# Stage loads issued by SyncE in place of GpSimd, and no transferred Strassen sums in the last gate unit

## The chip, the cores and the metric

The kernel runs on one core of a Trainium2 chip. The time is the device time of one execution in microseconds; of the kernel before three runs took 2368.52 to 2370.82 us, with a median of 2368.99.

A core has five engines that run side by side: TensorE (PE in the profile, its weight loads PEld), VectorE (DVE), ScalarE (ACT), GpSimd (POOL) and SyncE (SP). Each takes its own instructions in order. A transfer is issued by an engine: SP and POOL do it here, each in the order of its own program, and an issue that has to wait for a buffer or for other data holds back everything behind it on that engine.

## The reference

One decoder block over 256 tokens of width 4096, in float32. A normed input is projected to 20480 columns; these feed a pooling branch, a gated convolution branch and two gates; the branches are projected back, gated, merged, projected once more, added to the input and normed:

```python
h = rmsnorm(x, norm_w[l])
proj = jnp.einsum('bsd,de->bse', h, w_in[l])
u_p, z_p, u_c, b_c, c_c, z_c, g_logit = jnp.split(proj, SPLIT_POINTS, axis=-1)
y_pool = causal_multiscale_pool(u_p, pool_w[l], pool_scale[l]) * jax.nn.silu(z_p)
y_conv = causal_gated_shortconv(u_c, b_c, c_c, conv_w[l], conv_b[l]) * jax.nn.silu(z_c)
ys = jnp.stack([y_pool, y_conv], axis=2)
br = jnp.einsum('bsnc,ncd->bsnd', ys, w_branch[l])
gates = jax.nn.sigmoid(g_logit.reshape(b, s, N_BRANCHES, d) + gate_b[l])
merged = jnp.sum(gates * br, axis=2)
x = x + jnp.einsum('bsd,de->bse', merged, w_out[l])
return rmsnorm(x, final_norm_w)
```

## The kernel before, in words

**Units and steps.** The columns of the three projections are worked off in units of 1024: twelve units of `w_in` for the two branches (names beginning with `c` and `p`; two of these also do the pooling), eight gate units `g0_0`, `g1_0`, ... `g0_3`, `g1_3`, eight branch units `b0_0`, `b1_0`, ... `b1_3`, and four output units `o0` to `o3`. A unit goes through its inner dimension in steps of 256 (16 steps for `w_in` and the output, 8 for a branch). Each step loads one block of weights, 128 partitions x 2048 values, into one of the three buffers of `raw` (a "weight load" below, SP, line 87).

Products are made in three parts from a high and a low part of each operand, so every block of weights is split: ACT copies it rounded into the `ring`, DVE subtracts that from the block and writes the low part beside it. There are two kinds of steps. A P step multiplies the blocks as they are, with 24 matmuls. An S step uses a Strassen-like scheme with 21 matmuls; for it DVE first makes sums of the blocks: `V` (two sums of 128x512 in one instruction of 128x1024) and `W`, which are split into the ring as well. `place_of_sum` and the table `HELPED` (line 625) take the sum V off DVE: for the S steps listed there under a unit's name, SP loads one summand into a free half of `E` or `R`, and POOL issues a second transfer that adds the other summand to it (`move_add`, line 94). Then only three quarters of the weights have to go to `raw` (1536 columns), since the first quarter is used only in that sum. An entry is taken only if a place is free in time.

**The order.** Matmuls, preparations and transfers are written down by one program that goes through the steps: `run_step` writes a step's matmuls, and behind each group of them `pump` (line 1222) writes down weight loads and splits as far ahead as buffers and ring allow, up to three steps. Every 6 matmuls a `tick` writes one item of `queue` (the ends of units: joining the partial sums, sigmoids, stores) and one item of the fills. The order on each engine is that in which the program writes it down.

**Fills and stages.** The left operands of the branch units (y) and of the output units (m, the merged branches) don't fit beside those of `w_in`. They are stored in DRAM (`y_d`, `m_d`), and as soon as a place of an earlier operand in `arena` is free, one is fetched. `Fill.fetch` (line 942) loads 128x512 values (256 KB) into a stage; at least 8 ticks (`LANDING`, line 963) later `pop_fill` (line 965) writes down its split into `arena`, a copy by ACT and a subtraction by DVE, for an S operand with four small sums by DVE before. The stages are the second half of `sa`, the tile `sb`, and until the second step of `b0_0` two quarters of `Y`. 19 such loads are of y: they begin in `g0_3` and most of them come in `g1_3` and `b0_0`, a few later; 12 are of m, from `b0_3` to the beginning of `o0`.

**The end of the last gate unit.** When an S unit's last S step is not its last step, its shared banks close early: the four instructions of `joins` (line 452) combine them in `R`, and then POOL adds the gate's bias (`gate_b`, 1024 KB to 128 partitions) to `R` by an adding transfer. `combine` (line 481) leaves 12 ticks and lets DVE add `E` to `R`. Of the gate units `g1_3` alone has its last S step before its last step.

In the profile nearly every DVE sum has line 72, every ACT copy line 69, SP's loads line 87, POOL's loads and stores line 91, and its adding transfers line 94; matmuls have line 1301. So the tiles' names tell the instructions apart.

Of the kernel before, what the change touches and what calls it, by code (L numbers as in the profile page):

```python
# [56 lines left out]
def hybrid_block(ctx: ExitStack, tc: tile.TileContext, x, x_t, norm_t, w_first, w_in, pool_w, pool_scale,  # L57
# [28 lines left out]
    def load(dst, src):  # L86
        return pin(nc.sync.dma_start(dst, src))  # L87

    def move(dst, src):

        return pin(nc.gpsimd.dma_start(dst, src))
# [72 lines left out]
    def flat(q):  # L164
        return q.rearrange("p o c -> p (o c)")
# [456 lines left out]

    few = NS_X - NB
    LAST_FIRST = ('cc0',)
    HELPED = {'cc0': (1, 2, 4, 5), 'cz0': (1, 2, 5), 'cb0': (1, 2, 4, 5, 7, 8), 'cu1': (1, 2, 4, 5, 7, 8), 'cc1': (1, 2, 4, 7, 8), 'cz1': (1, 2, 4, 5, 7), 'cb1': (1, 2, 4, 5), 'pz0': (1, 4, 5, 7), 'pu0': (1, 2, 4, 5, 7), 'pz1': (1, 4, 5, 6, 8), 'pu1': (1, 2, 4, 5, 7), 'g0_0': (1, 2, 4, 5, 7), 'g1_3': (1, 2, 5), 'g1_0': (1, 2, 4, 5, 8), 'g0_1': (1, 2, 4, 5, 6, 7), 'g1_1': (1, 4, 5, 7, 8), 'g0_2': (1, 2, 3, 4, 5, 7, 8), 'g1_2': (1, 2, 4, 5, 7, 8), 'g0_3': (1, 2, 4, 5, 7, 8), 'o0': (1, 2, 4, 5, 6), 'o1': (1, 2, 4, 5, 7), 'o2': (0, 1, 2, 4, 5), 'o3': (0, 2, 4, 5)}
    PLACES = {
# [308 lines left out]
    class Fill:  # L935
# [5 lines left out]

        def fetch(self, st):
            self.at, self.st = now[0], st
            move(flat(st), self.src)

        def fill(self):
            if self.o.kind == "P":
# [331 lines left out]
    for u in units:  # L1279
        for k, s in enumerate(t for t in u.steps if t.kind == "S"):  # L1280
            if k in HELPED.get(u.name, ()):
                helped.append(s)
# [315 lines left out]
```

## Time and profile before

| | |
|---|---|
| median of 3 runs | 2368.99 us (2368.52 to 2370.82) |
| the profiled execution | 2368.59 us |
| its span, first to last instruction | 2366.9 us |
| mean granted TensorE clock | 0.998 |
| PE busy | 2349.3 us (99%) |
| DVE busy | 2192.1 us (93%) |
| ACT busy | 1423.9 us (60%) |
| POOL busy | 138.3 us (6%) |
| transfers | 596.44 MB, 499.98 by SP's queue and 93.60 by POOL's |

The profile is of one execution. Its rows give the start of an instruction in us from the span's start, its duration, the engine, the line, the operation, what it writes and reads, and in brackets how long the engine was idle before it and what ended the wait. PE counts as busy while a matmul is under way; each overlaps the next, so that the spacing of their starts tells more than their durations. For a transfer the time to landing counts from its issue.

### The profile page before, as it was taken

To read this page: it belongs to the slowest core of one execution; us is meant where nothing else is said; L and a number is where in the kernel's file an instruction comes from. 1 tells how busy PE (TensorE), PEld (TensorE's weight loads), DVE (VectorE), ACT (ScalarE), POOL (GpSimd) and SP (SyncE) were. 2 spreads that over 40 slices of the span, in tenths; PEclk is the share of its full clock that TensorE was granted. 3 is DMA by queue.
4 is the path that set the end of the run, shared out by engine and by line. 5 is a ranking of instruction groups with operands and counts; after the bars stand their busy time and mean duration, and the time that the engine had idled before them with its cause. 6 is when DMAs were issued, how large, how long until landed. Compare 5 with 4: busy or idle time off the path is not lost.

```text
span 2366.9 us, 28142 instructions
## 1 busy us (share of the span) xinstructions
PE 2349.3 (99%) x10465; PEld 1943.7 (82%) x10465; DVE 2192.1 (93%) x2259; ACT 1423.9 (60%) x1481; POOL 138.3 (6%) x207
## 2 busy tenths in 40 slices
PE   9999999999999999999999999999999999999998
PEld 7888888888888888888888888888878888888886
DVE  8999999999999989989999999989899899899998
ACT  7565665656556656656666656565665566566555
POOL 0000000000001001000000000001100001000000
PEclk9999999999999999999999999999999999999999
DMA  8566678877777668656887898887866668778877
GB/s 337 179 235 212 242 273 255 262 238 232 258 260 244 226 226 253 232 211 229 273 284 246 276 284 258 257 307 243 273 230 233 243 241 282 250 229 286 264 244 274
DMA packets 107754, 596.44 MB, mean 252 GB/s; under 512 B 11424, under 2 KB 11680, under 8 KB 53984
## 3 DMA queue, kind: packets, MB, share of 16 engines
q1 hardware_dynamic: 84848, 499.98, 58.2%
q0 software_dynamic: 22336, 93.60, 16.7%
q8 instruction: 82, 1.34, 0.2%
q10 hardware_dynamic: 432, 1.07, 0.1%
q14 instruction: 56, 0.46, 0.1%
HBM read 562.09 MB, written 25.17 MB: 248 GB/s over the span
## 4 chain that ended last, share of the span: by engine, by line
PE 96%; DVE 2%; DMA 1%; ACT 1%; issue 0%; SPq 0%; DVEq 0%; ACTq 0%
PE sums L1301 70%; PE shared L1301 24%; PE shared L809 1%; DVE ring L72 1%; PE shared L528 1%; DMA raw<-in_w_in_dram 0%; ACT ring L69 0%; DVE R L72 0%; DMA raw<-in_w_out_dram 0%; DVE W L72 0%; PE shared L788 0%; SPq L87 0%; DVE V L72 0%; DVE arena L72 0%; PE shared L789 0%
## 5 line engine op out<-in xcount | busy, mean ns | idle before, releaser
L1301 PE MATMUL sums<-ring,arena 128*128 128x512 f32 x7551 | 1788.6, 390 | 4.7 <-DVE ring L72 2.5
L1301 PEld LDWEIGHTS sums<-ring,arena 128*128 128x128 f32 x7551 | 1414.2, 188 | 299.8 <-DVE ring L72 3.7
L72 DVE TENSOR_TENSOR ring<-raw,ring 128x1024 fp32r<-128x1024 f32 (+3 forms) x689 | 937.7, 1388 | 81.0 <-ACT ring L69 79.4
L69 ACT ACTIVATE ring<-raw 128x1024 fp32r<-128x1024 f32 (+3 forms) x689 | 794.3, 1186 | 234.5 <-PE sums L1301 126.9
L1301 PE MATMUL shared<-ring,arena 128*128 128x512 f32 x2556 | 646.9, 390 | 1.1 <-DVE ring L72 1.0
L1301 PEld LDWEIGHTS shared<-ring,arena 128*128 128x128 f32 x2556 | 480.5, 188 | 102.2 <-DVE ring L72 2.4
L69 ACT ACTIVATE ring<-W 128x1024 fp32r<-128x1024 f32 x213 | 226.3, 1062 | 396.3 <-DVE W L72 325.8
L72 DVE TENSOR_TENSOR ring<-W,ring 128x1024 fp32r<-128x1024 f32 x213 | 261.1, 1226 | 20.6 <-ACT ring L69 8.9
L69 ACT ACTIVATE ring<-V 128x1024 fp32r<-128x1024 f32 x154 | 163.1, 1059 | 171.8 <-DVE V L72 138.9
L72 DVE TENSOR_TENSOR V<-raw 128x1024 f32<-128x1024 f32 x154 | 187.8, 1219 | 10.4 <-DMA raw<-in_w_in_dram 7.6
L72 DVE TENSOR_TENSOR ring<-V,ring 128x1024 fp32r<-128x1024 f32 x154 | 187.8, 1219 | 3.5 <-ACT ring L69 3.5
L72 DVE TENSOR_TENSOR W<-W,raw 128x512 f32<-128x512 f32 x213 | 146.2, 687 | 0.0
L72 DVE TENSOR_TENSOR W<-V,raw 128x512 f32<-128x512 f32 x154 | 106.4, 691 | 4.6
L72 DVE TENSOR_TENSOR R<-R,E 128x1024 f32<-128x1024 f32 (+1 forms) x49 | 77.4, 1592 | 8.9 <-DMA R<-in_gate_b_dram 5.3
L94 POOL DMA_DIRECT2D E<-in_w_in_dram x34 | 29.5, 869 | 593.9 <-DMA E<-in_w_in_dram 311.5
L72 DVE TENSOR_TENSOR R<-R,shared 128x512 f32<-128x512 f32 x87 | 59.6, 685 | 2.2 <-ACT R L69 0.3
L69 ACT ACTIVATE arena<-sa 128x512 fp32r<-128x512 f32 (+2 forms) x49 | 25.5, 554 | 57.3 <-DVE sa L72 57.2
L72 DVE TENSOR_TENSOR ring<-E,ring 128x1024 fp32r<-128x1024 f32 x45 | 55.2, 1226 | 1.5 <-ACT ring L69 1.5
L69 ACT ACTIVATE E<-sums,rin 128x512 f32<-128x512 f32 x76 | 49.2, 681 | 11.7 <-PE sums L1301 11.7
L69 ACT ACTIVATE ring<-E 128x1024 fp32r<-128x1024 f32 x45 | 47.1, 1046 | 6.1 <-PE shared L1301 2.8
L72 DVE TENSOR_TENSOR W<-E,raw 128x512 f32<-128x512 f32 x41 | 28.3, 691 | 4.7 <-DMA E<-in_w_in_dram 2.3
L72 DVE TENSOR_TENSOR ring<-R,ring 128x1024 fp32r<-128x1024 f32 (+1 forms) x20 | 26.7, 1336 | 4.0 <-ACT ring L69 4.0
(146 smaller groups left out, 629.8 us busy)
## 6 DMA issues: line engine op xcount, KB each, us to landing
raw<-in_w_in_dram SPq DMA_DIRECT2D x267, 1024.0 KB, 4.9
raw<-in_w_branch_dram SPq DMA_DIRECT2D x64, 1024.0 KB, 5.4
raw<-in_w_out_dram SPq DMA_DIRECT2D x56, 1024.0 KB, 5.8
raw<-in_w_in_dram SPq DMA_DIRECT2D x51, 768.0 KB, 6.4
E<-in_w_in_dram SPq DMA_DIRECT2D x34, 512.0 KB, 7.1
E<-in_w_in_dram POOLq DMA_DIRECT2D x34, 512.0 KB, 9.4
R<-in_w_in_dram SPq DMA_DIRECT2D x17, 512.0 KB, 7.6
R<-in_w_in_dram POOLq DMA_DIRECT2D x17, 512.0 KB, 8.7
```

The costliest lines, as they stand in the source:

```text
L69: return pin(nc.scalar.activation(dst, src, func, **kw))
L72: return pin(nc.vector.tensor_tensor(out=dst, in0=a, in1=b, op=op))
L94: return pin(nc.gpsimd.dma_start(dst, src, accum_op=ALU.add))
L528: pin(nc.tensor.transpose(shared(j)[:, i * T + t * P:i * T + (t + 1) * P], src[:, t, c:c + P], ident))
L809: pin(nc.tensor.matmul(o, a[:, k, ts], b[:, k], start=(k, i) == (0, 0), stop=(k, i) == (3, 2)))
L1301: pin(nc.tensor.matmul(ps, lhs, rhs, start=n == 0, stop=n == u.total[b] - 1))
```

## The change

Two lines are changed. A fill's fetch is issued by SP (`load`) and no longer by POOL (`move`), for all 31 stage loads. And the table `HELPED` loses its entry for `g1_3`, so that all S steps of that unit have their sum V made by DVE and load whole blocks of weights. (The table stands on one line in the code.)

```diff
     HELPED = {'cc0': (1, 2, 4, 5),
...
               'g0_0': (1, 2, 4, 5, 7),
-              'g1_3': (1, 2, 5),
               'g1_0': (1, 2, 4, 5, 8),
...
         def fetch(self, st):
             self.at, self.st = now[0], st
-            move(flat(st), self.src)
+            load(flat(st), self.src)
```

`load` and `move` differ in the issuing engine alone:

```python
def load(dst, src):
    return pin(nc.sync.dma_start(dst, src))

def move(dst, src):

    return pin(nc.gpsimd.dma_start(dst, src))
```

More of the change, by code (lines that the diff above doesn't have):

```diff
@@ L624, in hybrid_block @@
     LAST_FIRST = ('cc0',)
-    HELPED = {'cc0': (1, 2, 4, 5), 'cz0': (1, 2, 5), 'cb0': (1, 2, 4, 5, 7, 8), 'cu1': (1, 2, 4, 5, 7, 8), 'cc1': (1, 2, 4, 7, 8), 'cz1': (1, 2, 4, 5, 7), 'cb1': (1, 2, 4, 5), 'pz0': (1, 4, 5, 7), 'pu0': (1, 2, 4, 5, 7), 'pz1': (1, 4, 5, 6, 8), 'pu1': (1, 2, 4, 5, 7), 'g0_0': (1, 2, 4, 5, 7), 'g1_3': (1, 2, 5), 'g1_0': (1, 2, 4, 5, 8), 'g0_1': (1, 2, 4, 5, 6, 7), 'g1_1': (1, 4, 5, 7, 8), 'g0_2': (1, 2, 3, 4, 5, 7, 8), 'g1_2': (1, 2, 4, 5, 7, 8), 'g0_3': (1, 2, 4, 5, 7, 8), 'o0': (1, 2, 4, 5, 6), 'o1': (1, 2, 4, 5, 7), 'o2': (0, 1, 2, 4, 5), 'o3': (0, 2, 4, 5)}
+    HELPED = {'cc0': (1, 2, 4, 5), 'cz0': (1, 2, 5), 'cb0': (1, 2, 4, 5, 7, 8), 'cu1': (1, 2, 4, 5, 7, 8), 'cc1': (1, 2, 4, 7, 8), 'cz1': (1, 2, 4, 5, 7), 'cb1': (1, 2, 4, 5), 'pz0': (1, 4, 5, 7), 'pu0': (1, 2, 4, 5, 7), 'pz1': (1, 4, 5, 6, 8), 'pu1': (1, 2, 4, 5, 7), 'g0_0': (1, 2, 4, 5, 7), 'g1_0': (1, 2, 4, 5, 8), 'g0_1': (1, 2, 4, 5, 6, 7), 'g1_1': (1, 4, 5, 7, 8), 'g0_2': (1, 2, 3, 4, 5, 7, 8), 'g1_2': (1, 2, 4, 5, 7, 8), 'g0_3': (1, 2, 4, 5, 7, 8), 'o0': (1, 2, 4, 5, 6), 'o1': (1, 2, 4, 5, 7), 'o2': (0, 1, 2, 4, 5), 'o3': (0, 2, 4, 5)}
     PLACES = {
```

## The prediction

> **What bounds the kernel now.** I read the page first, then the busy time by stretches of 60 us, and then the instructions in order of time where PE was idle, engine by engine.
>
> ```profile
> PE 2349.3 (99%) x10465; PEld 1943.7 (82%) x10465; DVE 2192.1 (93%) x2259; ACT 1423.9 (60%) x1481; POOL 138.3 (6%) x207
> ```
>
> PE is the engine that is full. The stretches tell where it isn't:
>
> ```profile
> core 0 of [0], span 2366.9 us
> core 0: us, PE busy (x) PEld busy (x) DVE busy (x) ACT busy (x) POOL busy (x), PEclk, DMA share, GB/s
> 1560.00:1620.00 60.00, 60.00 (x266) 49.71 (x265) 53.12 (x51) 36.09 (x38) 4.68 (x6) 1.00 0.79 257
> 1620.00:1680.00 60.00, 58.41 (x254) 46.96 (x253) 52.04 (x62) 36.36 (x40) 5.72 (x10) 1.00 0.74 260
> 1680.00:1740.00 60.00, 56.40 (x239) 45.63 (x238) 51.35 (x65) 35.10 (x44) 5.53 (x9) 0.97 0.75 262
> 1740.00:1800.00 60.00, 60.00 (x274) 49.89 (x273) 57.10 (x54) 34.11 (x37) 2.60 (x5) 1.00 0.62 218
> ```
>
> Of the span of 2366.9 us PE is idle for 17.6. A full stretch holds 266 wide matmuls, 0.226 us each. Apart from the first and the last microseconds of the program, PE falls behind only between 1620 and 1740, that is in the last gate unit `g1_3` and the first branch unit `b0_0`, where the stages of y are fetched. What PE does there:
>
> ```profile
> 1649.08 2.48 PE L1301 MATMUL shared<-ring,arena 128*128 128x512 f32 x9
> ...
> 1659.41 2.81 PE L1301 MATMUL sums<-ring,arena 128*128 128x512 f32 x11 [0.49 <-DVE ring L72]
> ```
>
> ```profile
> 1717.56 2.20 PE L1301 MATMUL sums<-ring,arena 128*128 128x512 f32 x9
> 1721.22 0.50 PE L1301 MATMUL sums<-ring,arena 128*128 128x512 f32 x1 [1.46 <-ACT ring L69]
> 1723.74 0.83 PE L1301 MATMUL sums<-ring,arena 128*128 128x512 f32 x2 [2.02 <-DVE ring L72]
> 1724.38 4.44 PE L1301 MATMUL shared<-ring,arena 128*128 128x512 f32 x12
> 1728.65 1.55 PE L1301 MATMUL sums<-ring,arena 128*128 128x512 f32 x6
> ```
>
> First stall: 34 matmuls start between 1649.08 and 1659.41 and need 34 x 0.226 = 7.7 us; they took 10.3, so 2.6 are lost, all waiting for DVE. Second stall: 24 matmuls from 1717.56 to 1728.65 need 5.4 and took 11.1, so 5.7 are lost. Part of these is clock:
>
> ```profile
> 1720.82:1724.24 3.42, 1.00 (x3) 0.63 (x4) 3.42 (x5) 3.42 (x5) 0.53 (x1) 1.00 0.17 72
> 1724.24:1727.65 3.41, 3.41 (x10) 2.63 (x9) 3.41 (x5) 3.41 (x6) 0.00 (x0) 0.50 0.88 322
> ```
>
> After 3.4 us with PE busy for 1.0 the clock is granted at 0.50 for 3.41 us, which costs half of that, 1.7. So the second stall is 4.0 of waiting and 1.7 of clock. These 8.3 us are all that better fetching can win.
>
> **Why DVE is late there.** DVE's waits for transfers, in order of time:
>
> ```profile
> 1636.29 1.02 DVE L72 TENSOR_TENSOR sa<-sa 128x128 f32<-128x128 f32 x4 [3.71 <-DMA sa<-y_d]
> ...
> 1703.89 1.23 DVE L72 TENSOR_TENSOR R<-R,E 128x1024 f32<-128x1024 f32 x1 [5.25 <-DMA R<-in_gate_b_dram]
> ```
>
> 3.71 us go to a stage load, the fourth of y's, called the late load below; 5.25 to the gate's bias, which a DMA adds to R. Before the first stall stands the one, before the second the other. POOL, which issues both, tells why the stage load is late:
>
> ```profile
> 1624.50 0.90 POOL L94 DMA_DIRECT2D E<-in_w_in_dram  x1 [12.44 <-DMA E<-in_w_in_dram]
> 1625.07 0.89 POOL L91 DMA_DIRECT2D sa<-y_d  x1
> ```
>
> POOL stood 12.44 us at the adding transfer for the Strassen sum of `g1_3`, whose first half SyncE was still loading, and the stage load was queued behind it.
>
> **The change, part by part.** On POOL, from the end of `g0_3` on (one piece of the difference; E is the place of the Strassen sum):
>
> ```order
>  L94 DMA R<-in_w_in_dram 128x1024
> -L91 DMA sa<-y_d 128x512
>  L94 DMA R<-in_gate_b_dram 128x2x1024
> -L91 DMA sa<-y_d 128x512
> -L91 DMA sb<-y_d 128x512
> -L94 DMA E<-in_w_in_dram 128x1024
> -L91 DMA sa<-y_d 128x512
>  L91 DMA gates_d<-R 128x2048
> ```
>
> The blocking transfer and all stage loads leave; R's bias and the gate's store remain. Only one of the three entries for `g1_3` was ever taken, so one transfer pair goes. On SP at the same place, before and then changed:
>
> ```order
> L87 DMA raw<-in_w_in_dram 128x1536
> L87 DMA raw<-in_w_in_dram 128x2048 x8
> L87 DMA E<-in_w_in_dram 128x2x512
> L87 DMA raw<-in_w_in_dram 128x2048 x3
> L87 DMA raw<-in_w_in_dram 128x1536
> ```
>
> ```order
> L87 DMA raw<-in_w_in_dram 128x2048
> L87 DMA sb<-y_d 128x512
> L87 DMA raw<-in_w_in_dram 128x2048 x2
> L87 DMA sa<-y_d 128x512
> L87 DMA Y<-y_d 128x512
> L87 DMA raw<-in_w_in_dram 128x2048
> ```
>
> The late load (the `sa` here) now follows two weight loads, and the `x1536` weight behind E becomes a whole one. On DVE one piece:
>
> ```order
> +L72 TENSOR_TENSOR V<-raw 128x1024
>  L72 TENSOR_TENSOR arena<-sb,arena 128x512
> -L72 TENSOR_TENSOR W<-E,raw 128x512
> -L72 TENSOR_TENSOR ring<-raw,ring 128x3x512
> -L72 TENSOR_TENSOR W<-W,raw 128x512
> -L72 TENSOR_TENSOR ring<-E,ring 128x2x512
> +L72 TENSOR_TENSOR W<-V,raw 128x512
> ```
>
> One sum is DVE's again; the rest only reads V for E. Its price, and the durations of the transfers concerned (whole page, then the window 1687 to 1706):
>
> ```profile
> L72 DVE TENSOR_TENSOR V<-raw 128x1024 f32<-128x1024 f32 x154 | 187.8, 1219 | 10.4 <-DMA raw<-in_w_in_dram 7.6
> ```
>
> ```profile
> R<-in_gate_b_dram POOLq DMA_DIRECT2D x7, 1024.0 KB, 12.5
> ```
>
> ```profile
> raw<-in_w_branch_dram SPq DMA_DIRECT2D x4, 1024.0 KB, 10.3
> R<-in_gate_b_dram POOLq DMA_DIRECT2D x1, 1024.0 KB, 16.1
> ```
>
> Step 1, the late load: SP can issue it when DVE has split the stage's last contents, at 1622.6, and DVE wants it at 1636.29 - 3.71 = 1632.6. (The first row is DVE's; the others are transfers of the window 1606 to 1636.)
>
> ```profile
> 1621.95 0.68 DVE L72 TENSOR_TENSOR arena<-sa,arena 128x512 fp32r<-128x512 f32 x1
> ```
>
> ```profile
> sa<-y_d POOLq DMA_DIRECT2D x2, 256.0 KB, 9.5
> sb<-y_d POOLq DMA_DIRECT2D x2, 256.0 KB, 12.2
> ```
>
> With 9.5 us it lands at 1632.1, in time; with 12.2 DVE waits 2.2. DVE gains between 1.5 and 3.7; I take 3.71, since fewer bytes move there than before (E's two transfers of 512 KB go, 256 KB of weights come).
>
> Step 2, the added sum: DVE loses 1.22. Net 2.49 at 1650. PE waits directly for DVE there, so 2.5 of the first stall's 2.6 go.
>
> Step 3, three stage loads on POOL shared the DMA engines with weights that ACT then waited for, and DVE for ACT:
>
> ```profile
> 1661.48 0.54 POOL L91 DMA_DIRECT2D sb<-y_d  x1
> 1662.02 1.06 POOL L91 DMA_DIRECT2D Y<-y_d  x2
> ```
>
> ```profile
> 1674.19 1.23 DVE L72 TENSOR_TENSOR ring<-raw,ring 128x1024 fp32r<-128x1024 f32 x1 [1.39 <-ACT ring L69]
> ```
>
> ```profile
> ACT ring L69 <- DMA raw<-in_w_branch_dram: 6.7, 3, 3.9
> ```
>
> (The last is of ACT's waits from 1660 to 1705.) In the new order on SP these three come after the third weight of the branches, so the first weights are ahead of them:
>
> ```order
> L87 DMA raw<-in_w_branch_dram 128x2048 x3
> L87 DMA sb<-y_d 128x512
> L87 DMA Y<-y_d 128x512 x2
> L87 DMA raw<-in_w_branch_dram 128x2048 x2
> L87 DMA sa<-y_d 128x512
> ```
>
> Before, SP had only the 64 weights in a row there. DVE's 1.39 goes (bounds 0 and 1.39). So DVE finishes R 2.49 + 1.39 = 3.88 us earlier, and POOL, which issues the bias then, does it at 1683.9:
>
> ```profile
> 1687.75 1.23 POOL L94 DMA_DIRECT2D R<-in_gate_b_dram  x1 [1.31 <-DVE R L72]
> ```
>
> Step 4, the bias transfer: between the usual 12.5 us and this place's 16.1. No stage load stands around it in POOL's queue any more, but SP's queue beside it stays full. I take the middle, 14.3; DVE gains another 1.8, 5.7 in all.
>
> Step 5, the second stall: its 4.0 us of waiting shrink by what DVE gains over PE, 5.7 - 2.5 = 3.2, to 0.8. The first stall, 2.6 us in several pauses, left the clock at 1.00 (stretch 1620 above), so I take the 1.7 us of half clock as gone (bounds 0 and 1.7).
>
> Step 6, at nothing: SP's issues and waits for the 31 loads (19 of y, 12 of m). In 1540 to 1760 SP waits almost always, for DVE to free a weight buffer:
>
> ```profile
> SPq L87 <- DVE W L72: 106.5, 18, 12.8
> SPq L87 <- DVE ring L72: 95.7, 24, 8.3
> ```
>
> A stage load waits for a DVE instruction that stands earlier in the program than the one the next weight load waits for, so it is let through first. If that cover failed, the weights behind it would be late (third rival). The loads of m come where ACT itself waits for PE to free the ring (window 1940 to 2060), so PE has its lead and their 256 KB each cost nothing:
>
> ```profile
> ACT ring L69 <- PE sums L1301: 17.6, 11, 3.7
> ```
>
> Sum: 2.5 + 3.2 + 1.7 = 7.4 us. The profiled execution took 2368.59 (span 2366.9 and 1.7 around it), 0.4 under the median of 2368.99. So 2361.2 against it, 2361.6 against the median.
>
> **The rivals.** First, the bias lands no sooner. For it: the DMA engines are full there (10.3 us for a weight against a median of 4.9 for the page's 267 of `w_in`), and few bytes go.
>
> ```profile
> raw<-in_w_in_dram SPq DMA_DIRECT2D x267, 1024.0 KB, 4.9
> ```
>
> Then DVE gains 3.88, the second stall keeps 4.0 - 1.4 = 2.6 of waiting, and the clock may still drop: 2.5 + 1.4 = 3.9 us, 2365.1. The Trainium skill (DMA: Bandwidth & Descriptors, Issuing engines are not separate DMA queues) says that transfers of all issuing engines run on the same 16 engines, and that issuing from several saves only the issuing time. By that rule this rival would be the outcome; the full engines agree with it, of the 12.44 us block in POOL's order it does not speak.
>
> Second, the change doesn't free DVE: on SP the late load stands behind two weight loads, and if it takes 12.2 us, DVE still waits 2.2 and with the added sum gains 0.3. For it speaks the crowd of that stretch, against it that the crowd shrinks. If step 3 fails too, the stalls stay nearly whole: 2368.7.
>
> Third, slower: SP holds the weights at a stage load whose buffer isn't free. POOL did:
>
> ```profile
> 1698.94 0.54 POOL L91 DMA_DIRECT2D sb<-y_d  x1 [8.98 <-DVE arena L72]
> ```
>
> In the new order this load stands before the tenth weight of the branches. If SP stands 9.0 us there and nothing covers it, PE loses 9.0 less the 2.5 gained: 2368.99 + 6.5 = 2375.5. It decides from a hold of 7.2 us on (2.5 + 4.7); against it is that SP waits for DVE there anyway.
>
> **How the numbers follow.** My forecast (5 to 8.3 us won) has 0.57, the first rival 0.17, the second 0.12, the third 0.14. 0.2% is 4.7 us, about what a measurement of this kernel can tell from no change. A little of the first rival, where the clock holds, counts as faster (3.9 + 1.7): faster 0.60, same 0.26, slower 0.14. The low end is all 8.3 us gone (2360.7) and one more for what I read off by tenths; the high end takes in the first two rivals and as much again: 2359.6 to 2369.5. The forecast's own range is 2359.9 to 2364.2.
>
> **What would show it.** Right: DVE's 3.71 wait for the stage is gone, POOL has no 12 us wait at E, PE's waits before 1660 vanish, the clock stays at 1.00 near 1720, DVE's wait for the bias is under 4 us. Wrong: ACT waits for weights grow beyond 6.7 us between 1660 and 1705, or new waits of PE from 1740 on.

## The result, and the profile after

The changed kernel takes 2361.11 us (2360.6 to 2362.27), the kernel before on the same chip 2368.99 (2368.52 to 2370.88). The ratio is 0.9965, with a 95% interval of 0.9954 to 0.9976: faster by 7.9 us, forecast were 7.4. The profiled execution took 2360.96 us, its span is 2359.2.

The page's line on the engines, after. DVE has one instruction more, the sum `V`, and POOL 32 fewer: 31 stage loads and one adding transfer.

```profile
PE 2346.9 (99%) x10465; PEld 1943.4 (82%) x10465; DVE 2192.6 (93%) x2260; ACT 1424.7 (60%) x1481; POOL 121.0 (5%) x175
```

The stretches of 60 us, after. PE was busy for 58.41 and 56.40 us in them before; now both are full, and the second is back at a clock of 1.00:

```profile
1620.00:1680.00 60.00, 60.00 (x266) 49.47 (x265) 57.07 (x68) 40.53 (x46) 0.59 (x1) 1.00 0.69 258
1680.00:1740.00 60.00, 59.98 (x264) 49.03 (x263) 53.71 (x65) 33.67 (x41) 2.31 (x3) 1.00 0.74 259
```

PE's waits over the whole program, after. Both rows lie in the first 100 us of the program; behind these PE has no wait left that the view shows:

```profile
PE shared L1065 <- DVE rout L1070: 1.1, 1, 1.1
PE sums L1301 <- DVE ring L72: 0.3, 1, 0.3
```

At the place of the second stall PE's timeline, after, shows no bracket, and twelve matmuls take 2.9 us where they took 4.44 at half clock. Only the group of twelve ahead of them is still a little late: from its start to the next one's are 3.01 us (1714.81 to 1717.82), and 12 x 0.226 are 2.7, so 0.3 are lost in gaps too short for a bracket.

```profile
1714.81 3.17 PE L1301 MATMUL sums<-ring,arena 128*128 128x512 f32 x12
1717.82 2.90 PE L1301 MATMUL shared<-ring,arena 128*128 128x512 f32 x12
1720.56 8.78 PE L1301 MATMUL sums<-ring,arena 128*128 128x512 f32 x38
```

The cause, in the timelines of SP, DVE and POOL, after. SP issues the late load at 1622.87; DVE takes it at 1632.81 without a wait (no bracket), and still waits 2.54 us for the gate's bias, where it waited 5.25:

```profile
1622.87 0.33 SPq L87 DMA_DIRECT2D sa<-y_d  x1
...
1632.81 1.01 DVE L72 TENSOR_TENSOR sa<-sa 128x128 f32<-128x128 f32 x4
...
1684.14 1.17 POOL L94 DMA_DIRECT2D R<-in_gate_b_dram  x1 [61.06 <-ACT ring L69]
...
1697.40 1.23 DVE L72 TENSOR_TENSOR R<-R,E 128x1024 f32<-128x1024 f32 x1 [2.54 <-DMA R<-in_gate_b_dram]
```

**A measure inside the trace.** The profile of a second execution of the changed kernel (number 11 below) has a span of 2361.8 us against 2359.2, a difference larger than some experiments are to tell, and part of it lies at the start and the end. So the tables below use a stretch of PE's work that all these kernels share: from the group of nine matmuls near 1614, ahead of all the changes, to the last group of the program. Before (first fence) it takes 2355.36 - 1613.69 = 741.67 us, after (second fence) 2347.53 - 1614.00 = 733.53. That is 8.1 us less, and the two stalls had been read as 8.3.

```profile
1613.69 2.20 PE L1301 MATMUL shared<-ring,arena 128*128 128x512 f32 x9
...
2355.36 0.88 PE L1534 MATMUL shared<-ring,arena 128*128 128x256 f32 x6
```

```profile
1614.00 2.20 PE L1301 MATMUL shared<-ring,arena 128*128 128x512 f32 x9
...
2347.53 0.88 PE L1534 MATMUL shared<-ring,arena 128*128 128x256 f32 x6
```

PE had lost another 0.4 us between the two stalls, in gaps too short for a bracket. The same 171 matmuls there, before (first fence) and after (second fence):

```profile
1674.30 39.34 PE L1301 MATMUL sums<-ring,arena 128*128 128x512 f32 x171
```

```profile
1671.97 38.92 PE L1301 MATMUL sums<-ring,arena 128*128 128x512 f32 x171
```

### The profile page after: what moved, and what is told of

It is laid out like the page before. It is cut to its first block, busy times and chain, and to the rows that moved or that the text cites. A ratio compares the mean times of both kernels' runs of the same rounds, so it can differ in the third digit from the quotient of the medians.

```text
span 2359.2 us, 28140 instructions
## 1 busy us (share of the span) xinstructions
PE 2346.9 (99%) x10465; PEld 1943.4 (82%) x10465; DVE 2192.6 (93%) x2260; ACT 1424.7 (60%) x1481; POOL 121.0 (5%) x175
## 4 chain that ended last, share of the span: by engine, by line
PE 99%; DMA 0%; DVE 0%; SPq 0%; ACT 0%; issue 0%; DVEq 0%
PE sums L1301 72%; PE shared L1301 25%; PE shared L809 1%; PE shared L528 1%; DMA raw<-in_w_in_dram 0%; PE shared L788 0%; SPq L87 0%; PE shared L789 0%; PE shared L791 0%; SPq L162 0%; DVE ring L72 0%; ACT ring L69 0%; ACT V L69 0%; PE shared L790 0%; PE sums L1534 0%
```

## The experiments

Eleven kernels in three groups, each group beside the kernel before on one chip (its medians there: 2369.48, 2367.91 and 2370.06 us). "Gain" is by the measure above; the last two columns are the transfer of `g1_3`'s bias and DVE's wait for it.

| kernel | median us | ratio to before, interval | gain | bias | DVE waits |
|---|---|---|---|---|---|
| before | 2368.99 | | | 16.1 | 5.3 |
| changed | 2361.11 | 0.9965 [0.9954, 0.9976] | 8.1 | 13.2 | 2.5 |
| 1 table alone | 2365.71 | 0.9987 [0.9978, 0.9996] | 2.7 | 16.0 | 5.0 |
| 2 queue alone | 2361.3 | 0.9969 [0.9958, 0.9981] | 8.4 | 14.2 | 2.4 |
| 3 add later | 2365.09 | 0.9982 [0.9973, 0.9991] | 4.1 | 15.9 | 5.3 |
| 4 no bias | 2363.39 | 0.9975 [0.9966, 0.9984] | 4.1 | none | none |
| 5 m on POOL | 2361.6 | 0.9969 [0.9957, 0.9982] | 6.5 | 14.3 | 3.7 |
| 6 one ahead of the bias | 2362.4 | 0.9973 [0.9962, 0.9985] | 7.2 | 14.6 | 3.5 |
| 7 four near 1660 | 2363.47 | 0.9978 [0.9969, 0.9988] | 6.3 | 13.7 | 4.1 |
| 8 add later, no bias | 2360.54 | 0.9964 [0.9951, 0.9977] | 8.9 | none | none |
| 9 one behind the bias | 2363.07 | 0.9969 [0.9958, 0.998] | 6.4 | 15.0 | 4.3 |
| 10 four around the bias | 2364.51 | 0.9979 [0.9969, 0.9988] | 6.0 | 15.8 | 4.4 |
| 11 changed, again | 2361.8 | 0.9966 [0.9952, 0.998] | 7.1 | 14.1 | 3.4 |

The last row sets the scale: the changed kernel's own two profiles differ by 1.1 us in the gain, the later arrival of the bias among it. The gain is of one execution each. By the medians the kernels gain up to 2.0 us more or less than this column says (kernel 4: 6.1, kernel 7: 4.4), so a difference of one or two microseconds between two rows isn't shown by the column alone.

### The two parts alone

**1, the table alone**: the entry of `g1_3` goes, all stage loads stay on POOL.

```diff
-    HELPED = {..., 'g0_0': (1, 2, 4, 5, 7), 'g1_3': (1, 2, 5), 'g1_0': (1, 2, 4, 5, 8), ...}
+    HELPED = {..., 'g0_0': (1, 2, 4, 5, 7), 'g1_0': (1, 2, 4, 5, 8), ...}
```

> The table's entry for g1_3 is gone, the stage loads stay on POOL. My theory: the 12.44 us wait of POOL goes and with it DVE's 3.71, less 1.22 for the added sum, so the first stall (2.6 us of PE) nearly vanishes. Three stage loads still share the engines with the branch weights near 1660, DVE keeps its 1.39, and the bias still follows a stage load and takes about 16 us, so the second stall of 5.7 stays: 2366.5 us. Rival (what counts is E's bytes, which crowd the DMA engines): loads and bias get faster everywhere, nearly the whole gain, about 2361.5 us. Rival (only the queue counts): 2369.

Measured: a gain of 2.7 us, about the first stall. POOL's hold at E is gone and with it DVE's wait for the late load. The second stall stays, and behind it a stretch of half clock. PE's waits in this kernel; the first two are the second stall, the other two lie ahead of all the changes:

```profile
PE sums L1301 <- DVE ring L72: 2.0, 1, 2.0
PE sums L1301 <- ACT ring L69: 1.3, 1, 1.3
PE shared L1065 <- DVE rout L1070: 1.1, 1, 1.1
PE shared L1301 <- DVE ring L72: 0.4, 1, 0.4
```

**2, the queue alone**: SP issues the stage loads, the table keeps its entry.

```diff
-            move(flat(st), self.src)
+            load(flat(st), self.src)
```

> All 31 stage loads are issued by SP, the table keeps g1_3, so the Strassen sum still goes through E. My theory: the late load no longer stands behind the adding transfer, DVE gains its 3.71 without paying 1.22, the bias has POOL's queue to itself: both stalls vanish, 2361 us, at most 0.5 from the changed kernel. Rival (bytes): as many bytes as before move, the crowd stays, most of the gain is missing, 2367. Rival (the rule that the issuing engine saves only issuing time): 2369.

Measured: the whole gain, 8.4 us. POOL stands at the adding transfer as before, even a little longer, but no stage load is queued behind it. POOL's timeline in this kernel:

```profile
1621.20 0.91 POOL L94 DMA_DIRECT2D E<-in_w_in_dram  x1 [13.10 <-DMA E<-in_w_in_dram]
1622.45 0.57 POOL L91 DMA_DIRECT2D gates_d<-R  x1 [0.34 <-issue]
1682.70 1.19 POOL L94 DMA_DIRECT2D R<-in_gate_b_dram  x1 [59.68 <-DVE R L72]
```

So the two parts don't add: both free the late load, 2.7 and 8.4 against 8.1 together. Once SP issues the loads, nothing measurable is left for the table's entry to give.

### The first stall's cause by itself

**3, add later**: the kernel before, in which POOL's adding transfer for E is written down a few weight loads later. In POOL's order this one row moves, to behind the late load, the gate's store and two more stage loads (three loads in all, not four as the expectation has it). No transfer is added, removed or put on another engine.

```diff
-                    adding.append((state["nl"] + WAIT, t, v, w[:, NH:3 * NH]))
+                    adding.append((state["nl"] + (4 if t.host.name == "g1_3" else WAIT), t, v, w[:, NH:3 * NH]))
```

> The kernel before with one row moved on POOL: the adding transfer of g1_3 is issued three places later in SP's order, so four stage loads and a store stand ahead of it in place of behind it. Same transfers, same engines, same bytes. My theory (the order of POOL's queue makes the late load late): DVE's 3.71 goes, the first stall goes, the second stays or is a little shorter: 2366.4 us. Rivals (bytes, or the queue's kind): no change, 2369.

Measured: 4.1 us. The hold at E, the 3.71 us and the first stall are gone with the order alone. It is 1.4 more than table alone gains: there DVE makes the added sum, at 1.22 us, here it doesn't. (By the medians the two are only 0.6 apart.) What is left is the second stall, some 0.8 us shorter (PE waits 0.62 us for ACT in it, before 1.46), and its half clock, by windows of 3.4 us in this kernel:

```profile
1716.94:1720.36 3.42, 1.16 (x4) 0.76 (x5) 3.42 (x5) 3.42 (x5) 0.54 (x1) 1.00 0.26 72
1720.36:1723.77 3.41, 3.41 (x10) 2.63 (x9) 3.41 (x5) 3.41 (x7) 0.00 (x0) 0.50 0.85 329
```

### The second stall's cause by itself

**4, no bias**: the kernel before without `g1_3`'s bias transfer.

```diff
-        more = [] if u.added is None or not early else [lambda: move_add(u.dst, u.added)]
+        more = [] if u.added is None or not early or u.name == "g1_3" else [lambda: move_add(u.dst, u.added)]
```

> The kernel before without the adding transfer of the gate's bias in g1_3 (this unit's bias is left out). My theory (the bias' landing sets the second stall): DVE's 5.25 us wait goes, down to the 2 us or so for which the weights are late there too; the second stall's 4.0 us of waiting go to 1 or less and the half clock with them; the first stall stays at 2.6: 2363.8 us. Rival (the second stall comes from the first, or from late weights): DVE waits for the weights as long, 2368.5 us.

Measured: 4.1 us. The second stall and the half clock are gone. The first stall stays, and in this execution it is longer: 46 matmuls from 1646.85 to 1661.43 need 46 x 0.226 = 10.4 us and took 14.6, so 4.2 are lost in place of 2.6 (DVE waited 4.25 us for the late load here, and 1.02 for a weight ahead of it). That is why the gain stays below the 5.7 of the second stall; the profiled execution, 2364.98 us, is also 1.6 slower than the kernel's median. PE's waits in this kernel; the 2.2 and 0.5 of the 0.8 are the first stall, the rest is from the first 100 us of the program:

```profile
PE shared L1301 <- DVE ring L72: 2.2, 2, 1.2
PE shared L1065 <- DVE rout L1070: 1.1, 1, 1.1
PE sums L1301 <- DVE ring L72: 0.8, 2, 0.5
```

**8, add later and no bias**: both edits together, all stage loads still on POOL.

> The kernel before with the adding transfer of the Strassen sum issued three places later and without the bias transfer of g1_3 (this unit's bias is left out); all stage loads on POOL. My theory (the two stalls have these two causes and no third): both stalls go, 2361 us with all loads on POOL. Rival (POOL's stage loads themselves cost): 2363 or more.

Measured: 8.9 us, which are the 8.3 of both stalls, the 0.4 between them and 0.2 that aren't placed. That kernels 3 and 4 apart give nearly as much, 4.1 + 4.1 = 8.2, is chance: kernel 3 gains some of the second stall too, and kernel 4 loses by its longer first one. PE's waits in this kernel, both from the first 100 us of the program:

```profile
PE shared L1065 <- DVE rout L1070: 1.1, 1, 1.1
PE sums L1301 <- DVE ring L72: 0.2, 1, 0.2
```

The stalls have these two causes and no third; and a better arrival of the bias could give the changed kernel at most about a microsecond more, which these runs wouldn't tell from nothing.

### Which of the moved loads matter

The next five are the changed kernel with some loads back on POOL. Four count the fetches and pick some by number (5 picks by operand):

```diff
-            load(flat(st), self.src)
+            fetched.append(self); (move if len(fetched) in (8, 9, 10, 11) else load)(flat(st), self.src)
```

**5, m on POOL**: the 12 loads of m (`(load if self.o not in m_ops else move)`).

> The changed kernel with the twelve loads of m back on POOL. My theory (step 6: they are covered by PE's lead on either queue): no difference, 2361.1 us, within 0.5. Rival (part of the gain is made by m's loads): 2363 or more.

Measured: 2361.6. PE has one wait of 0.3 us after 1740, so for m the issuing engine costs nothing that this run shows. Most of the 1.6 us less of gain lies at the bias, which landed later here (PE waits 1.1 us for DVE at 1718), as in the second profile of the changed kernel, though nothing near it was edited.

**7, four near 1660** (fetches 8 to 11, as in the diff).

> The changed kernel with the four stage loads near 1660 us back on POOL, none of them near the bias. My theory (step 3): they share the engines with the first branch weights again, ACT waits for a weight near 1670, DVE loses the 1.39 us, the bias is issued 1.2 later, PE waits 1.2 at the second stall: 2362.3 us, or 2364 if the half clock follows. Rival (these loads cost nothing wherever they are): 2361.1, and the 1.39 came from elsewhere.

Measured: 2363.47, gain 6.3: between the two expected times, with the clock at 1.00 throughout. DVE's waits for ACT tell step 3 directly. First the two waits of this kernel, then the one that the changed kernel has there:

```profile
1671.38 1.23 DVE L72 TENSOR_TENSOR ring<-raw,ring 128x1024 fp32r<-128x1024 f32 x1 [1.35 <-ACT ring L69]
1675.71 1.23 DVE L72 TENSOR_TENSOR ring<-raw,ring 128x1024 fp32r<-128x1024 f32 x1 [1.04 <-ACT ring L69]
```

```profile
1674.56 1.23 DVE L72 TENSOR_TENSOR ring<-raw,ring 128x1024 fp32r<-128x1024 f32 x1 [1.03 <-ACT ring L69]
```

Kernels 1 and 3, whose loads are on POOL, have both (1.31 and 1.35 us for the first); kernel 2, whose loads are on SP, has the second alone. The 1.39 us of the kernel before belong to these loads. ACT's waits for branch weights say the same, more loosely: 6.5 us from 1660 to 1705 here, 3.8 and 5.0 in the two profiles of the changed kernel.

**6, one ahead of the bias** (fetch 13, which POOL issues just before it).

> The changed kernel with one stage load back on POOL, the one that stands directly ahead of the bias there. My theory (a stage load ahead of the bias in its own queue makes it late, step 4): the bias takes 15 to 16 us in place of 13.2, DVE waits 2 us longer for it, and since the changed kernel has no reserve at the second stall PE waits 2 us, with the half clock 3.7: 2363 to 2364.8 us. Rival (the bias is slow from SP's weights beside it and from nothing else): 13 us and 2361.1.

Measured: 14.6 us for the bias, 2362.4. It went less far than expected: one load ahead of the bias isn't what makes 16 us.

**9, one behind the bias** (fetch 14), **10, four around the bias** (fetches 12 to 15, two on each side), and **11, the changed kernel again** beside them.

> The changed kernel with one stage load back on GpSimd: the 14th fetch, the Y load that GpSimd issues right behind the gate bias of g1_3. It cannot delay the bias's issue (about 1684). If a stage load that GpSimd issues behind the bias stretches its transfer, the bias takes 15 us or more, the VectorE wait for it rises from 2.5 to about 4.5 us, TensorE waits 1 to 2 us and the time is 2362 to 2363.5. If it does not, the bias takes 13.2 to 14.3 us as with all loads on SyncE, and the time is 2361.2.

> The changed kernel with the four stage loads around the gate bias of g1_3 (two ahead of it, two behind it) back on GpSimd. If the 16 us of the bias in the kernel before come from these neighbours on its own queue, the bias takes 15.5 to 16.1 us here, VectorE waits about 5 us for it, TensorE waits 2 to 3 us near 1718, perhaps with the half clock behind it, and the time is 2363.5 to 2366. If the queue does not matter, the bias takes 13.2 to 14.6 us and the time is 2361.2 to 2362.4.

> The changed kernel once more, beside the two others on the same chip, as their measure: 2361.1 within 0.6, the bias 13.2 to 14.3 us.

Transfers issued from 1682 to 1688, in the order 9, 10, 11 (the last column is the time to landing in us):

```profile
R<-in_gate_b_dram POOLq DMA_DIRECT2D x1, 1024.0 KB, 15.0
...
Y<-y_d POOLq DMA_DIRECT2D x1, 256.0 KB, 16.0
```

```profile
R<-in_gate_b_dram POOLq DMA_DIRECT2D x1, 1024.0 KB, 15.8
...
Y<-y_d POOLq DMA_DIRECT2D x1, 256.0 KB, 15.9
```

```profile
R<-in_gate_b_dram POOLq DMA_DIRECT2D x1, 1024.0 KB, 14.1
Y<-y_d SPq DMA_DIRECT2D x1, 256.0 KB, 12.1
```

Kernels 9 and 10 came as the first of their two expectations has it; the time of kernel 11 lies 0.1 us beyond the 0.6 that it was given. With four stage loads back around it, the bias is at 15.8 us, nearly what it took with all of them on POOL (15.9 to 16.1); with one behind, at 15.0; with none near it on POOL, 13.2 to 14.3 over five profiles (the changed kernel's two and kernels 2, 5 and 7). So the neighbours on the bias's own queue make it slow. (POOL also issues three of the four up to 1.1 us earlier than SP does, `Y` at 1685.62 in kernel 10 and at 1686.67 in the changed kernel; this is not separated from the queue.) PE's longest waits in the middle, in the order 9, 10, 11, follow the arrival:

```profile
1719.21 0.73 PE L1301 MATMUL sums<-ring,arena 128*128 128x512 f32 x2 [1.80 <-DVE ring L72]
```

```profile
1719.55 0.74 PE L1301 MATMUL sums<-ring,arena 128*128 128x512 f32 x2 [2.01 <-DVE ring L72]
```

```profile
1718.11 0.73 PE L1301 MATMUL sums<-ring,arena 128*128 128x512 f32 x2 [0.89 <-DVE ring L72]
```

The ratios of 10 and 11 to the kernel before overlap in their intervals. Compared with each other, on one chip, the two do differ: seven of the nine runs of kernel 10 take longer than each of the five of kernel 11, and the medians are 2.7 us apart. By what way a neighbour slows the bias, through the descriptors that POOL writes or through the order in which the queue is served, was not told apart.

## Why the prediction was right

The time came 0.5 us under the forecast, inside the forecast's own range, and none of the rivals came about. By its steps:

**Steps 1 to 3** can be tested together, since each shifts the moment at which DVE is done with R and POOL issues the bias. Counted from the fixed group of matmuls near 1614, the issue comes earlier than before by:

| kernel | by the steps | measured |
|---|---|---|
| changed | 3.71 - 1.22 + 1.39 = 3.88 | 3.92 |
| table alone (steps 1 and 2) | 3.71 - 1.22 = 2.49 | 2.58 |
| add later (step 1) | 3.71 | 3.84 |
| queue alone (steps 1 and 3) | 3.71 + 1.39 = 5.10 | 5.15 |
| four near 1660 (steps 1 and 2) | 3.71 - 1.22 = 2.49 | 2.50 |

For the changed kernel the measured number is (1687.75 - 1613.69) - (1684.14 - 1614.00) = 3.92; the others come from the same two rows of their traces. Each step has the size that was read off the profile before, to about 0.1 us. (Kernels 5, 9 and 11 have 3.9 like the changed one; 6 and 10 have 4.3, and why is open.) Of step 1, the late load's own time of 6.8 us was better than the 9.5 taken, with no effect, since 9.5 was in time already.

**Step 4** is the term that was mis-sized: 14.3 us for the bias was a middle between two rows, and it took 13.2 in the profile. The reason given, that no stage load stands around it in POOL's queue any more, is what kernel 10 shows. Over five profiles it took 13.2 to 14.3, so the value taken lies at the slow end of what the kernel does. Counted from the fixed group, DVE came to the sum of R and E (1703.89 - 1613.69) - (1697.40 - 1614.00) = 6.8 us earlier than before, where 5.7 were forecast.

**Step 5** followed from it: 0.8 us of waiting were to remain at the second stall, 0.3 did, in the group of twelve shown above. In the second profile, with the bias at 14.1 us, the wait is the 0.89 quoted above. The 1.7 us of half clock went, as taken. Against the forecast's 7.4, the 8.1 of the trace are these 0.5 and the 0.4 between the stalls, less some 0.2 of small delays elsewhere. So the prediction had it wrong that the 8.3 us of the two stalls are all that better fetching can win. That the median came within 0.5 us of the forecast is in part luck: the two profiles of the changed kernel differ by 1.1 us, and by as much the bias missed the value taken.

**Step 6** held: PE has no wait after 1740, and SP's order didn't make PE wait for weights. SP did wait for DVE's splits into `arena`, which free the stages, six times between 1600 and 1720, 4.8 us at most and 10.8 in all, and none of it reached PE. The load before which the third rival saw SP stand for 9.0 us is issued at 1694.90 at once, and SP then waits for DVE's W, as was argued against this rival (SP's timeline, after):

```profile
1694.30 0.33 SPq L87 DMA_DIRECT2D raw<-in_w_branch_dram  x1
1694.90 0.33 SPq L87 DMA_DIRECT2D sb<-y_d  x1
1703.84 0.33 SPq L87 DMA_DIRECT2D raw<-in_w_branch_dram  x1
```

**The first rival's rule**, of the Trainium skill (DMA: Bandwidth & Descriptors, Issuing engines are not separate DMA queues), does not carry here. Kernel 2 moves the same transfers to another issuing engine and wins 8.4 us in the trace, where POOL spends some 0.5 us on issuing a stage load. It leaves out two things. One is the order on the issuing engine: kernel 3 moves a single row past others and wins 4.1. The same page of the Trainium skill says elsewhere (Anatomy of one DMA, SWDGE (gpsimd) path) that waits are made by the issuing engine before it issues, and the 12.44 us at E are such a wait. The other is the bias, which the moved loads slowed on its queue. What the rule says of shared DMA engines agrees with the trace: in no profile did the bias come down to its usual 12.5 us there, beside the weights.

**The second rival** would have needed the late load to take 12.2 us on SP; it took 6.8.

## What to carry to other kernels

On an engine that issues transfers, look for the issue that waits long and ask what stands behind it: here an adding transfer that nobody was in a hurry for held a 256 KB load that everybody waited for, and moving either of the two freed it. Follow the shift further along the chain before pricing it, since more than half of the gain lay 60 us later, where the same engine's lead decided when the next transfer was issued, and 1.7 us of it in the clock that fell behind the stall. Two edits that free the same wait do not add up, so try each alone.

## What the runs showed of the hardware

- The bias, a 1 MB adding transfer on POOL's queue, took 13.2 to 14.3 us with the 256 KB stage loads on SP's queue, and 15.9 to 16.1 with them on its own, with the branch weights on SP's queue beside it in both cases. A 256 KB load issued right behind it took 15.9 to 16.4 us on POOL's queue and 11.3 to 12.4 on SP's.
- The clock fell to 0.50 for 3.4 us after stretches of 3.4 us in which PE had been busy for 1.00 (before), 1.16 (kernel 3) and 1.39 us (kernel 1, the first fence below), and not after one with 1.85 (kernel 7, from 1716.74 to 1720.16) or 2.02 (kernel 10, the second fence). PE needn't be idle for such a fall. Where between 1.39 and 1.85 it is decided, these cases don't tell.
- It matters where such a stretch lies. Taken from 1716.14 to 1719.55, kernel 10 has 1.40 us of busy time too, and keeps its clock. The stretches above lie on a fixed raster that the traces' records of the clock show: it stayed unchanged for 1720.32 us (before), 1716.90 (kernel 1) and 1713.49 (kernel 3) ahead of the fall and for 631.47 behind it in all three, which are 504, 503, 502 and 185 times 3.4133 us. For kernels 7 and 10, whose clock doesn't fall there, the raster is counted back from the clock's last change, at 2355.03 and 2353.82.

```profile
1720.07:1723.48 3.41, 1.39 (x6) 0.94 (x6) 3.41 (x6) 3.41 (x5) 0.54 (x1) 1.00 0.15 24
1723.48:1726.90 3.42, 3.42 (x10) 2.65 (x9) 3.42 (x4) 3.42 (x6) 0.00 (x0) 0.50 0.92 357
```

```profile
1715.52:1718.94 3.42, 2.02 (x9) 1.18 (x7) 2.88 (x4) 3.42 (x5) 0.00 (x0) 1.00 0.50 208
1718.94:1722.35 3.41, 2.80 (x12) 2.35 (x13) 3.41 (x5) 3.41 (x6) 0.53 (x1) 1.00 0.56 183
```
